# An encoder kernel on one core: pieces of turned heads issued by ScalarE, a query block moved ahead of the values, two more heads turned by DMA

## The chip, the cores and the metric

The kernel runs on one core of one Trainium2 chip. The metric is the device time of one execution in microseconds (us); lower is better. A core has TensorE (PE, with its weight loads PEld), VectorE (DVE), ScalarE (ACT), GpSimd (POOL) and SyncE (SP). Each takes its instructions in the order in which they were laid down, and waits on semaphores for the others. A DMA is issued by one of these instruction streams (here by SP, by POOL, and at the very end by ACT) and carried out by 16 DMA engines that all of them share. A row whose engine ends in "q" (SPq, ACTq) is the issuing itself, done by the engine's sequencer.

## The reference

Two encoder layers work on 256 tokens of width 2048. Both have four cross-attention heads into 256 memory tokens. The first layer has twelve heads of neighbourhood attention with a bias; the second has twelve query heads over four key and value heads, with queries and keys normalised per head and rotated by position. All of the changed parts lie in the attention of the two layers:

```
n = rms_norm(h, attn_norm[1])
z = n @ b_w_in[0]
q, k, v, qm = split(z)
q = axial_rope(rms_norm(split_heads(q, 12), b_q_norm[0]))
k = axial_rope(rms_norm(split_heads(k, 4), b_k_norm[0]))
mix = gqa_block_attention(q, k, v)            # softmax(q k^T / sqrt(128)) v per head
cross = memory_attention(qm, km, vm)          # four heads into the memory tokens
h = h + concat([mix, cross]) @ w_o[1]
h = h + square(relu(rms_norm(h, mlp_norm[1]) @ w_up[1])) @ w_down[1]
```

## The kernel before

**Products.** Every fp32 matrix is split into two parts, hi (ScalarE rounds it, line 330) and lo (VectorE subtracts, line 331), and each product is made of three TensorE matmuls: hi·hi, lo·hi, hi·lo (lines 238, 241, 242 for blocks of 512 columns; 250 to 252 and 823 to 825 for blocks of 256). Weights come in chunks of 1 MB, loaded by SP (line 186) into three buffers (`raw`) and split in two halves; four buffers hold the hi and lo halves.

**Order.** The work is a list of grains, one per half of a chunk. A counter ticks once per grain. `later(n, f)` runs `f` n ticks on, so that attention work is written between the grains of the projections. From this written order and its own estimates of durations a planner lays out the final order of the instructions on each engine; the instructions wrapped in `pin` keep their written order.

**Attention of one head** has three steps. `attend` makes the scores on TensorE (lines 393 to 395), the maximum on VectorE (404), the exponential on ScalarE (406) and the scaling on VectorE (411). The second step turns the probabilities. It has two forms: with `attend2`, TensorE transposes four 128x128 squares (436) and the result is split; with `turned`, VectorE transposes 32x32 squares (417) and `moved` writes four pieces to DRAM (line 382, one DMA for each group of 32 partitions) and reads them back in the wanted order with one DMA from POOL (383); `attend2_turned` splits what came back (330 and 331, tile `pT`). `attend3` multiplies by the values (444 to 446). A list such as `blocks=(0, 6, 8)` says how many ticks after its begin each step is written.

**Second layer.** The plan before is: the memory queries and the keys together, the values (block 4 of the weights), then three blocks of four query heads (0, 1, 2), then the output projection `add_o(1)`, then the MLP. `normed_heads` squares the sums on ScalarE with the row's factor (1199), gets the head's factor on VectorE and POOL (337, 339), multiplies it by the row's factor on POOL (1202), scales on ScalarE (1205) and rotates on VectorE (1207 to 1215). `heads_turned` turns queries or keys through `moved`; `heads_T` does it on TensorE (1169). `HEADS_AT` has the tick, counted from the end of a block, at which each of its four heads begins. Of block 0 all four heads are turned by DMA, of block 1 the first two, of block 2 none.

**Output projection.** `add_o` makes four blocks of 512 columns, two at a time, each a sum over four chunks of its input: chunk 3 has the memory heads, chunks 0, 1 and 2 have heads 0 to 3, 4 to 7 and 8 to 11.

`moved` has one more caller, `turned_rows`, which turns the rows of the activations ahead of and behind the MLP.

Of the kernel before, what the change touches and what calls it, by code (L numbers as in the profile page):

```python
# [17 lines left out]
P = 128  # L18
# [73 lines left out]
def encoder_kernel(ctx: ExitStack, tc: tile.TileContext, t: dict, out: bass.AP):  # L92
# [126 lines left out]
    def later(n, fn, *args):  # L219
        pending.append((state["tick"] + n, fn, args))  # L220
# [152 lines left out]
        return s  # L373


    def moved(dst, src):

        f = dst.shape[-1]
        x = dram.tile([P, 4, f], F32, tag=f"turn{f}", bufs=4, name="turn")
        to = x.rearrange("(b r) a f -> a r b f", r=32)  # L380
        for a in range(4):
            nc.sync.dma_start(to[a], src[32 * a : 32 * a + 32])
        nc.gpsimd.dma_start(dst, x)

    def scores(name):
# [28 lines left out]
    def turned(sc):  # L414

        x = scores("sc_t").rearrange("p a b -> p (a b)")
        nc.vector.transpose(x.rearrange("p (b k s j) -> p s k b j", b=4, k=2, s=2),
                            sc.rearrange("p s (k b r) -> p s k b r", k=2, b=4))
        back = sc.rearrange("p a b -> p (a b)").rearrange("p (a f) -> p a f", a=4)
        moved(back, x.rearrange("p (b f) -> p b f", b=4))  # L420
        return back

    def attend2_turned(back, o=0):
# [365 lines left out]
    def add_o(layer):  # L789
        first, second, third, late = 3, 0, 1, 2  # L790
        for n in (0, 2):
            if n:
                order = [(b, c) for b in range(2) for c in range(4)]
            elif layer:
                order = [(b, c) for c in (first, second, third, late) for b in range(2)]
            else:
                order = [(b, c) for b in range(2) for c in (first, second)]
                order += [(b, c) for c in (third, late) for b in range(2)]
            add_ms([([t[f"w_o{layer}"][nb * 4 + c] for c in range(4)], o_done(layer, nb)) for nb in (n, n + 1)],
                   parts_of("cat"), order)  # L800
            if n == 0 and layer == 1:
                last = [halves_of(w) for w in plan[-4:]]
                del plan[-4:]
                for two in (last[:2], last[2:]):
                    plan.extend(x[hf] for hf in range(2) for x in two)
# [280 lines left out]
    def down_done(layer, nb):  # L1086
        def f(w):
            for i in range(NT):
                add_scaled(h[:, i, nb * 512 : (nb + 1) * 512], w.ps[i], box["inv"][:, i : i + 1])
            for i in range(NT):  # L1090
                sum_squares(2 * layer + 1, i, nb)
            if layer == 1:
                later(1, times_gf, nb)
                return
            if nb == 0:
                box["nT"] = wide("nT1", 480)
            if nb == 3:
                closed("mlp")
                open_ring()
            later(1, turned_input, nb)  # L1100
            if nb == 3:

                def norm():
                    box["rstd"] = keep.tile([P, NT], F32, name="rstd1")
                    box["mean"] = mean_square(1, 4, "mean")
                    nc.gpsimd.tensor_tensor(box["rstd"], box["mean"], mhalf[:, :NT], op=ALU.pow)
                later(2, norm)
        return f

# [63 lines left out]
    def heads_turned(src, dst):  # L1173

        backs = []
        for i in range(NT):
            room = scores("h_t").rearrange("p a b -> p (a b)")
            nc.vector.transpose(room.rearrange("p (b k j) -> p k b j", b=4, k=4),
                                src[i].rearrange("p (k b r) -> p k b r", k=4, b=4))
            back = src[i].rearrange("p (a f) -> p a f", a=4)  # L1180
            moved(back, room.rearrange("p (b f) -> p b f", b=4))
            backs.append(back)

        def heads_landed():
            for i in range(NT):
                hi, lo = (dst[:, :, x * SEQ + i * P : x * SEQ + (i + 1) * P].rearrange("p k (a j) -> p k a j", a=4)
                          for x in range(2))
                split(hi, lo, backs[i].rearrange("p a (k j) -> p k a j", k=4))

        later(5, lambda: past(heads_landed, box["splits"][-1]))  # L1190

    def normed_heads(w):
        cg, sg = box["rope"]
        outs = []
        for i in range(NT):
            y2 = at.work.tile([P, 4, HD], F32, tag="b_y2", name="b_y2")
            ss = small.tile([P, 4], F32, tag="b_ss", name="b_ss")
            for j in range(4):
                nc.scalar.activation(y2[:, j, :], w.ps[i][:, j * HD : (j + 1) * HD], AF.Square,
                                     scale=box["rstd"][:, i : i + 1], accum_out=ss[:, j : j + 1])  # L1200
            r = rstd_of(ss, HD, "b_r")
            nc.gpsimd.tensor_scalar(r, r, box["rstd"][:, i : i + 1], None, op0=ALU.mult)
            y = at.work.tile([P, 4, HD], F32, tag="b_y", name="b_y")
            for j in range(4):
                nc.scalar.activation(y[:, j, :], w.ps[i][:, j * HD : (j + 1) * HD], AF.Copy, scale=r[:, j : j + 1])
            o = at.work.tile([P, 4, HD], F32, tag="b_o", bufs=3, name="b_o")
            nc.vector.tensor_tensor(o, y, cg[:, i, None, :].to_broadcast([P, 4, HD]), op=ALU.mult)
            yv = y.rearrange("p h (a b c) -> p h a b c", a=2, b=2)
            y2v = y2.rearrange("p h (a b c) -> p h a b c", a=2, b=2)
            sv = sg[:, i, :].rearrange("p (a b c) -> p a b c", a=2, b=2)  # L1210
            for a in range(2):
                for b in range(2):
                    nc.vector.tensor_tensor(y2v[:, :, a, b, :], yv[:, :, a, 1 - b, :],
                                            sv[:, None, a, b, :].to_broadcast([P, 4, 32]), op=ALU.mult)
            nc.vector.tensor_tensor(o, o, y2, op=ALU.add)
            outs.append(o.rearrange("p a b -> p (a b)"))
        return outs
# [8 lines left out]
        box["vb"] = values("values", "vb", 1)  # L1226
        put_values(box["vb"], w.ps, box["rstd"])

    HEADS_AT = (7, 9, 10, 12), (5, 6, 8, 9), (1, 3, 5, 6)

    def b_q_done(blk):
        def f(w):
# [4 lines left out]
            else:  # L1237
                later(1, heads_turned, outs, qT)
            kvs = [(blk * 4 + j) // (NH // NKV) for j in range(4)]
            jobs = [(qT[:, j, :], box["kT"][:, kv, :], None, head_of(box["vb"], kv), blk * 4 + j, box["cat"])  # L1240
                    for j, kv in enumerate(kvs)]
            n = (4, 2, 0)[blk]
            for j, job in enumerate(jobs):
                begin = HEADS_AT[blk][j]
                if j < n:
# [29 lines left out]
    for w in plan[-8:-5]:  # L1275
        w.early = True
    plan[-6].early = "last"
    add_m(blocks(4), parts_of("nT"), b_v_done)
    for blk in range(3):
        add_m(blocks(blk), parts_of("nT"), b_q_done(blk))  # L1280
    add_o(1)
    add_mlp(1)
# [131 lines left out]
```

## Time and profile before

| | |
|---|---|
| time, median of 3 runs | 2014.71 us (2011.62 to 2015.72) |
| time of the profiled execution | 2011.52 us |
| its span, first to last instruction | 2009.4 us |
| granted TensorE clock | 0.999 |
| busy: TensorE, VectorE, ScalarE, GpSimd | 1997.4, 1691.8, 1245.8, 142.7 us |

The shares of busy time are those of the whole span. The attention of the first layer lies between about 105 and 365 us, the projections and the attention of the second between about 1090 and 1290 us; the long stretches of MLP lie around them. The parts of the change touch only the two attention stretches.

### The profile page before, as it was taken

How to read it: one execution, taken by the hardware profiler on the slowest of the kernel's cores; microseconds unless marked ns; L12 is line 12 of the kernel's file. 1: busy time of each engine (PE TensorE's matmuls, PEld its weight loads, DVE VectorE, ACT ScalarE, POOL GpSimd, SP SyncE). 2: the span in 40 equal slices, each digit the busy share in tenths (PEclk: the TensorE clock that was granted, in tenths of full speed). 3: DMA queues.
4: the chain of work that ended last, by engine and by line, in shares of the span. 5: the costliest groups of instructions: out<-in, count | busy, mean ns of one | idle time of the engine just before them, and what ended most of it. 6: DMA issues, size and time to landing. Idle time of an engine off the chain costs nothing.

```text
span 2009.4 us, 32896 instructions
## 1 busy us (share of the span) xinstructions
PE 1997.4 (99%) x12945; PEld 1807.2 (90%) x12945; DVE 1691.8 (84%) x2080; ACT 1245.8 (62%) x1650; POOL 142.7 (7%) x185
## 2 busy tenths in 40 slices
PE   9999999999999999999999999999999999999998
PEld 8999999899999999999988888889999999999997
DVE  6767767669998999999998778768989999999896
ACT  6755555557666666666655567657666666666664
POOL 0000000000000000000000112000000000000000
PEclk9999999999999999999999999999999999999999
DMA  7766666847777787787767776557777777777763
GB/s 286 300 224 217 219 222 210 329 134 236 223 232 232 233 233 235 217 244 236 216 215 262 257 260 213 216 190 239 227 231 223 235 229 234 225 239 231 235 224 115
DMA packets 121626, 461.13 MB, mean 229 GB/s; under 512 B 13824, under 2 KB 36992, under 8 KB 88320
## 3 DMA queue, kind: packets, MB, share of 16 engines
q1 hardware_dynamic: 100080, 412.90, 61.3%
q0 software_dynamic: 20816, 45.10, 10.5%
q8 instruction: 101, 1.65, 0.3%
q10 hardware_dynamic: 576, 1.05, 0.1%
q14 instruction: 53, 0.43, 0.1%
HBM read 411.80 MB, written 17.83 MB: 214 GB/s over the span
## 4 chain that ended last, share of the span: by engine, by line
PE 94%; DMA 2%; DVE 2%; issue 1%; ACT 1%; SPq 0%; POOLq 0%; POOL 0%; DVEq 0%; ACTq 0%
PE ps_u L825 12%; PE ps_u L824 12%; PE ps_u L823 12%; PE p L942 9%; PE p L941 9%; PE p L940 9%; PE ps_m L242 7%; PE ps_m L238 7%; PE ps_m L241 7%; PE ps_s L250 3%; PE ps_s L252 3%; PE ps_s L251 3%; DMA sc<-turn 1%; DVE lo L331 1%; DMA raw<-in_w_o 1%
## 5 line engine op out<-in xcount | busy, mean ns | idle before, releaser
L825 PE MATMUL ps_u<-hT,ul 128*128 128x256 f32 x2048 | 566.4, 277 | 0.0
L824 PE MATMUL ps_u<-hT,uh 128*128 128x256 f32 x2048 | 565.1, 276 | 0.0
L823 PE MATMUL ps_u<-hT,uh 128*128 128x256 f32 x2048 | 564.5, 276 | 0.0
L330 ACT ACTIVATE uh<-raw_U 128x1024 fp32r<-128x1024 f32 x278 | 294.5, 1061 | 297.8 <-PE ps_u L824 280.3
L824 PEld LDWEIGHTS ps_u<-hT,uh 128*128 128x128 f32 x2048 | 384.3, 188 | 6.6
L823 PEld LDWEIGHTS ps_u<-hT,uh 128*128 128x128 f32 x2048 | 384.2, 188 | 5.6
L825 PEld LDWEIGHTS ps_u<-hT,ul 128*128 128x128 f32 x2048 | 384.3, 188 | 0.1
L331 DVE TENSOR_TENSOR ul<-raw_U,uh 128x1024 fp32r<-128x1024 f32 x278 | 337.6, 1219 | 25.5 <-ACT uh L330 25.5
L331 DVE TENSOR_TENSOR lo<-raw,hi 128x1024 fp32r<-128x1024 f32 (+1 forms) x224 | 265.1, 1191 | 102.5 <-ACT hi L330 99.9
L330 ACT ACTIVATE hi<-raw 128x1024 fp32r<-128x1024 f32 (+1 forms) x224 | 230.4, 1038 | 166.3 <-PE ps_m L242 65.7
L330 ACT ACTIVATE th<-t 128x2048 fp32r<-128x2048 f32 x112 | 215.1, 1921 | 115.4 <-PE p L942 108.8
L331 DVE TENSOR_TENSOR tl<-t,th 128x2048 fp32r<-128x2048 f32 x112 | 256.2, 2288 | 28.1 <-ACT th L330 27.4
L331 DVE TENSOR_TENSOR bl<-b,bh 128x1536 fp32r<-128x1536 f32 x112 | 196.3, 1753 | 5.3 <-ACT bh L330 5.3
L330 ACT ACTIVATE bh<-b 128x1536 fp32r<-128x1536 f32 x112 | 166.7, 1488 | 19.4 <-PE p L942 13.2
L920 POOL DMA_DIRECT2D t<-b x112 | 96.5, 861 | 1126.0 <-DVE t L919 419.7
L942 PE MATMUL p<-th,a_s 128*128 128x512 f32 x448 | 176.3, 393 | 0.0
L941 PE MATMUL p<-tl,a_s 128*128 128x512 f32 x448 | 176.0, 393 | 0.0
L940 PE MATMUL p<-th,a_s 128*128 128x512 f32 x448 | 159.1, 390 | 0.0
L942 PE MATMUL p<-bh,a_s 128*128 128x512 f32 x336 | 131.7, 392 | 0.0
L941 PE MATMUL p<-bl,a_s 128*128 128x512 f32 x336 | 131.1, 390 | 0.0
L251 PE MATMUL ps_s<-nT,hi 128*128 128x256 f32 x448 | 124.1, 277 | 0.0
L250 PE MATMUL ps_s<-nT,hi 128*128 128x256 f32 x448 | 123.9, 277 | 0.0
(288 smaller groups left out, 3790.0 us busy)
## 6 DMA issues: line engine op xcount, KB each, us to landing
raw_U<-in_w_up SPq DMA_DIRECT2D x128, 1024.0 KB, 7.5
b<-in_w_pair SPq DMA_DIRECT2D x112, 768.0 KB, 4.9
raw<-in_w_o SPq DMA_DIRECT2D x32, 1024.0 KB, 5.6
t<-in_w_pair SPq DMA_DIRECT2D x112, 256.0 KB, 3.3
t<-b POOLq DMA_DIRECT2D x112, 256.0 KB, 7.3
raw<-in_w_b SPq DMA_DIRECT2D x21, 1024.0 KB, 5.9
raw<-in_w_av SPq DMA_DIRECT2D x12, 1024.0 KB, 5.1
raw<-in_w_aq SPq DMA_DIRECT2D x12, 1024.0 KB, 5.1
```

Source lines behind the costliest of these rows:

```text
L238: first = nc.tensor.matmul(w.ps[i], ah, hi[:, s], start=st, stop=False)
L241: nc.tensor.matmul(w.ps[i], ah, lo[:, s], start=False, stop=False)
L250: nc.tensor.matmul(ps, hi[:, s], acts[:, k, :SEQ], start=k == 0, stop=False)
L251: nc.tensor.matmul(ps, hi[:, s], acts[:, k, SEQ:], start=False, stop=False)
L330: first = nc.scalar.activation(dst_hi, src, AF.Copy)
L331: return first, nc.vector.tensor_tensor(dst_lo, src, dst_hi.bitcast(F32), op=ALU.subtract)
L823: nc.tensor.matmul(ps, hi[:, s], acts[:, k, :SEQ], start=k == 0, stop=False)
L824: nc.tensor.matmul(ps, hi[:, s], acts[:, k, SEQ:], start=False, stop=False)
L825: nc.tensor.matmul(ps, lo[:, s], acts[:, k, :SEQ], start=False, stop=k == KT - 1)
L940: nc.tensor.matmul(ps, a[:, 0, ai, :], hi[:, s], start=begins, stop=False)
L941: nc.tensor.matmul(ps, a[:, 0, ai, :], lo[:, s], start=False, stop=False)
L942: nc.tensor.matmul(ps, a[:, 1, ai, :], hi[:, s], start=False, stop=ends)
```

## The change

Five things are changed together.

1. `moved` takes a queue. `turned` and `heads_turned` give it ScalarE's, so the four pieces of every turned head, query and key are issued by ScalarE; `turned_rows` keeps SP. The read back stays with POOL.
2. In the second layer query block 0 is projected ahead of the values (block 4). Since the values do not exist yet when its heads are written, they are looked up when the third step runs (`values_of`).
3. In block 1 all four heads are turned by DMA (before: two), and they begin at ticks 1, 3, 5, 7 instead of 5, 6, 8, 9.
4. `normed_heads` squares without the row's factor. The small constant of the norm is multiplied by the row's mean square once (`least`), so that the head's factor comes out whole and the multiplication on POOL (1202) is gone.
5. The first two blocks of the second layer's output projection take their first two chunks as in the first layer: both chunks of one block, then both of the other, instead of alternating.

```diff
-    def moved(dst, src):
+    def moved(dst, src, queue=nc.sync):
...
-            nc.sync.dma_start(to[a], src[32 * a : 32 * a + 32])
+            queue.dma_start(to[a], src[32 * a : 32 * a + 32])
         nc.gpsimd.dma_start(dst, x)
...
-        moved(back, x.rearrange("p (b f) -> p b f", b=4))
+        moved(back, x.rearrange("p (b f) -> p b f", b=4), nc.scalar)
...
-            elif layer:
-                order = [(b, c) for c in (first, second, third, late) for b in range(2)]
             else:
                 order = [(b, c) for b in range(2) for c in (first, second)]
                 order += [(b, c) for c in (third, late) for b in range(2)]
...
+                    box["least"] = keep.tile([P, NT], F32, name="least")
+                    nc.vector.tensor_scalar(box["least"], box["mean"], EPS, None, op0=ALU.mult)
...
-            moved(back, room.rearrange("p (b f) -> p b f", b=4))
+            moved(back, room.rearrange("p (b f) -> p b f", b=4), nc.scalar)
...
-                                     scale=box["rstd"][:, i : i + 1], accum_out=ss[:, j : j + 1])
-            r = rstd_of(ss, HD, "b_r")
-            nc.gpsimd.tensor_scalar(r, r, box["rstd"][:, i : i + 1], None, op0=ALU.mult)
+                                     accum_out=ss[:, j : j + 1])
+            v = small.tile([P, 4], F32, tag="rs_v", name="b_r_v")
+            nc.vector.tensor_scalar(v, ss, 1.0 / HD, box["least"][:, i : i + 1], op0=ALU.mult, op1=ALU.add)
+            r = small.tile([P, 4], F32, tag="rs_r", name="b_r_r")
+            nc.gpsimd.tensor_tensor(r, v, mhalf[:, :4], op=ALU.pow)
...
-    HEADS_AT = (7, 9, 10, 12), (5, 6, 8, 9), (1, 3, 5, 6)
+    HEADS_AT = (7, 9, 10, 12), (1, 3, 5, 7), (1, 3, 5, 6)
+
+    def values_of(kv):
+        return lambda part, kt: head_of(box["vb"], kv)(part, kt)
...
-            jobs = [(qT[:, j, :], box["kT"][:, kv, :], None, head_of(box["vb"], kv), blk * 4 + j, box["cat"])
+            jobs = [(qT[:, j, :], box["kT"][:, kv, :], None, values_of(kv), blk * 4 + j, box["cat"])
...
-            n = (4, 2, 0)[blk]
+            n = (4, 4, 0)[blk]
...
+    add_m(blocks(0), parts_of("nT"), b_q_done(0))
     add_m(blocks(4), parts_of("nT"), b_v_done)
-    for blk in range(3):
+    for blk in range(1, 3):
         add_m(blocks(blk), parts_of("nT"), b_q_done(blk))
```

## The prediction

> **What bounds the kernel now.** I read the page first: which engine is full, and who carries the chain that ended last.
>
> ```profile
> PE 1997.4 (99%) x12945; PEld 1807.2 (90%) x12945; DVE 1691.8 (84%) x2080; ACT 1245.8 (62%) x1650; POOL 142.7 (7%) x185
> PE 94%; DMA 2%; DVE 2%; issue 1%; ACT 1%; SPq 0%; POOLq 0%; POOL 0%; DVEq 0%; ACTq 0%
> ```
>
> TensorE is busy for 1997.4 us of a span of 2009.4 us, and 94% of the chain is TensorE. So 12 us are the most that could be saved without taking work from it. Next come its waits in the whole span, to see where these 12 us lie.
>
> ```profile
> PE unread L136 <- POOL idle L133: 1.3, 1, 1.3
> ...
> PE pt_h L1169 <- DVE b_o L1215: 0.3, 1, 0.3
> PE ps_m L241 <- DVE lo L331: 0.2, 1, 0.2
> ```
>
> Only the last two lie in the attention of the second layer; the rest is the start, and the tail behind the last matmul, which the change leaves alone. Then the windows of the stages: length, PE, PEld, DVE, ACT and POOL busy, clock, DMA share.
>
> ```profile
> 120.00:400.00 280.00, 279.94 (x1902) 257.31 (x1902) 198.17 (x294) 148.37 (x249) 9.33 (x17) 1.00 0.70 238
> 1152.00:1232.00 80.00, 80.00 (x393) 67.61 (x392) 62.81 (x112) 51.32 (x126) 12.75 (x18) 1.00 0.73 239
> 1208.00:1256.00 48.00, 47.45 (x253) 39.86 (x251) 44.97 (x93) 34.74 (x93) 9.16 (x12) 1.00 0.69 220
> ```
>
> In the first layer's attention TensorE is full. In the second it is full too, but for 0.55 us near 1248, where VectorE is at 94% (44.97 of 48). That crowd is the only place where the kernel waits for what the change moves.
>
> A busy TensorE can hide small gaps, since a matmul counts beyond the start of the next. So I read the starts there.
>
> ```profile
> 1247.59 0.62 PE L238 MATMUL ps_m<-hi,cat 128*128 128x512 f32 x2
> 1248.50 0.87 PE L1169 MATMUL pt_h<-ident,b_o 128*128 128x128 f32 x6 [0.29 <-DVE b_o L1215]
> 1249.13 0.48 PE L242 MATMUL ps_m<-hi,cat 128*128 128x512 f32 x1
> 1249.83 0.50 PE L241 MATMUL ps_m<-lo,cat 128*128 128x512 f32 x1 [0.22 <-DVE lo L331]
> 1250.17 0.40 PE L242 MATMUL ps_m<-hi,cat 128*128 128x512 f32 x1
> 1250.40 0.40 PE L238 MATMUL ps_m<-hi,cat 128*128 128x512 f32 x1
> ...
> 1253.68 0.60 PE L436 MATMUL pt_a<-ident,sc 128*128 128x128 f32 x4
> 1254.04 0.36 PE L393 MATMUL sc_ps<-kT,qT 128*128 128x256 f32 x1
> 1254.24 0.28 PE L394 MATMUL sc_ps<-kT,qT 128*128 128x256 f32 x1
> ...
> 1255.58 0.39 PE L241 MATMUL ps_m<-lo,cat 128*128 128x512 f32 x1
> 1256.07 0.73 PE L242 MATMUL ps_m<-hi,cat 128*128 128x512 f32 x2
> ...
> 1257.34 0.39 PE L241 MATMUL ps_m<-lo,cat 128*128 128x512 f32 x1
> 1257.72 0.39 PE L444 MATMUL av<-pT,vb 128*128 128x256 f32 x1
> ```
>
> From 1250.17 to 1250.40 one matmul of 512 columns takes 0.23 us. Beyond that, 1247.59 to 1248.50 holds 0.45 us of nothing (two matmuls, 0.46, in 0.91), 1249.13 to 1249.83 0.47, 1255.58 to 1256.07 0.26, 1257.34 to 1257.72 0.15: together **1.3 us**.
>
> **The change, part by part.**
>
> *Two more heads turned by DMA.* Eight transposes leave TensorE. Four start in 0.36 us (1253.68 to 1254.04), and the matmul behind them is followed after 0.20 instead of 0.12 us: 0.44 for four, so two heads give **-0.9 us**. VectorE gets two transposes more, priced below, in exchange for no other work; TensorE never waits for them if they have the six ticks that the plan leaves. If they are late, the third step stands in TensorE's queue and everything behind it waits; that price is inside the cases below.
>
> *Block 0 ahead of the values, block 1 earlier.* The head factors show when a block is through:
>
> ```profile
> 1133.94 2.02 POOL L339 TENSOR_TENSOR b_r_r<-b_r_v,mhalf 128x4 f32<-128x4 f32 x2
> 1180.57 1.04 POOL L339 TENSOR_TENSOR b_r_r<-b_r_v,mhalf 128x4 f32<-128x4 f32 x1 [2.45 <-DVE b_r_v L337]
> 1206.36 1.04 POOL L339 TENSOR_TENSOR b_r_r<-b_r_v,mhalf 128x4 f32<-128x4 f32 x1 [6.20 <-DVE b_r_v L337]
> ```
>
> Keys at 1134, block 0 at 1181, block 1 at 1206: a block is some 25 us. Block 0 then ends near 1156 and its four heads work from about 1170 to 1212 instead of from 1207 to 1245, out of the crowd. The last of block 1 is as late as before, but two ticks thinner. The 1.3 us of gaps are bounded by 0 (the crowd stays) and -1.3; I take all, **-1.3 us**, because the four heads that leave are a third of the second layer's query heads, and VectorE missed by only half a microsecond.
>
> *The weight loads.* SP now waits with the weights behind pieces:
>
> ```profile
> 1238.57 9.50 SPq L382 DMA_DIRECT2D turn<-sc_t  x8
> 1248.16 0.44 SPq L186 DMA_DIRECT2D raw<-in_w_o  x1
> 1253.50 1.06 ACT L330 ACTIVATE hi<-raw 128x1024 fp32r<-128x1024 f32 x1 [2.38 <-DMA raw<-in_w_o]
> ```
>
> A weight left at 1248.16, after eight pieces had held the queue for 9.5 us, and ScalarE had to wait for it until 1253.50. This goes. It is one of the causes of the 1.3 us and is not counted again. What is next in the load's way is the freeing of a `raw` buffer by VectorE.
>
> *Norms.* The POOL multiplication, the wider scalar operand on VectorE and `least` shift fractions of a microsecond on engines with room, outside the one gap at 1248.50, already counted: 0. Without that cover the whole of it is below 1 us.
>
> *Order of the projection.* The same matmuls; the second pair of sums starts two grains later, so the last block's sums have longer to be read. 0, since no wait names it; the weights wanted first are in the same queue order.
>
> *The issuing, on ScalarE.* This is the part that can cost. What one issue takes, on SP and on ScalarE:
>
> ```profile
> L382 SPq DMA_DIRECT2D turn<-sc_t x104: 302/432/1397, 113.9 to 1247.6; - x104
> 1997.50 1.34 ACT L1132 ACTIVATE h<-h,fin_r 128x512 f32<-128x512 f32 x2 [1.15 <-POOL fin_r L339]
> 1998.26 0.95 ACTq L1135 DMA_DIRECT2D out<-h  x2
> ```
>
> 0.43 us on SP, 0.48 on ScalarE (0.95 for two). ScalarE's first issue began at 1998.26, while its activation ran to 1998.84: the end of a running activation hides part of it. Moved are 28 turned heads (16, 12) and six halves of queries and keys, 34 x 4 = 136 issues, 65 us of ScalarE's stream. Ahead of each group it may also have to sit out VectorE's transpose, and then its splits queue up behind, for which TensorE waits in the end.
>
> First layer: 16 heads, 64 issues, 31 us, on top of 148.37 in 280: 64% busy, no bound. But the pieces may leave later, and some heads have little room between the turned tile and its first product:
>
> ```profile
> 140.79 0.69 DVE L331 TENSOR_TENSOR pT<-sc,pT 128x512 fp32r<-128x512 f32 x1 [2.41 <-ACT pT L330]
> 140.81 0.39 PE L444 MATMUL av<-pT,vm 128*128 128x256 f32 x1
> ...
> 289.14 0.69 DVE L331 TENSOR_TENSOR pT<-sc,pT 128x512 fp32r<-128x512 f32 x1 [2.94 <-ACT pT L330]
> 290.12 0.28 PE L444 MATMUL av<-pT,vl 128*128 128x256 f32 x1
> ```
>
> These are the first and the last of four heads with under 1 us. Below, the bound is 0: earlier pieces give nothing to a full TensorE. Above, each of the four is late by one whole split of 1.06 us: 4.2. I take the mean: ScalarE is busy 53% of the time, half a split is 0.53 us, so 0.28 for each of four, **+1.1 us**.
>
> Second layer, 1152 to 1232: ScalarE has 51.3 us. Four heads' `pT` and output splits come in, some 4.7 us (0.63 and about 0.55 each). Issues: 8 for the queries of block 0, 16 for the memory heads, 16 for block 0, 8 to 16 for block 1, so 48 to 56, by 0.43 to 0.48: 21 to 27 us. The sum is 77 to 83 of 80 us if nothing overlaps; with half an activation (0.3 us) hidden in each of 12 to 14 groups, 73 to 79. That is close. What protects TensorE is that the splits run ahead:
>
> ```profile
> ACT hi L330 <- PE ps_m L242: 65.7, 48, 3.0
> L330 ACT ACTIVATE hi<-raw 128x1024 fp32r<-128x1024 f32 (+1 forms) x224 | 230.4, 1038 | 166.3 <-PE ps_m L242 65.7
> ```
>
> ScalarE waits 48 times for TensorE to free a half: it has four halves, three of them ahead, each 12 matmuls of 0.23, so 8.3 us, less about 2.3 for the split itself. A lead of 6 us absorbs short holds. I take **0** here; the upper end is the rival's.
>
> *The sum.* -0.9 - 1.3 + 1.1 = -1.1 us, for the profiled execution 2011.5 - 1.1 = 2010.4. The median of the runs, 2014.71, stands 3.2 us above that execution, so the forecast for the median is **2013.6 us**.
>
> **Rivals.** *ScalarE becomes the bound (slower).* In 1152 to 1232, 83 us of work and issues, and waits in front of VectorE's transposes:
>
> ```profile
> L417 DVE STREAM_TRANSPOSE sc_t<-sc x26: 702/710/714, 113.1 to 1244.8; 128x512 f32<-128x512 f32 x26
> ```
>
> 14 groups of 0.71 are 9.9, so 93 of 80 us: 13 too many, less the lead of 6: +7, or +13 where the lead is used up already. It decides from the point where ScalarE's share of that window exceeds one. For it: the sum is within 10% of the window. Against it: ScalarE idles 36% there now, the planner sees the issues, and holds shorter than the lead cost nothing. Time 2013.6 + 7 = 2020.6, up to 2026.6.
>
> [...]
>
> *The change doesn't do what it says.* The planner lays the issues behind ScalarE's splits, the pieces leave a microsecond later, the heads are only shifted, and the crowd near 1248 stays: the transposes' -0.9 remain against +1.1 to +4.2. That is 2014.9 to 2018.0.
>
> *Clearly faster.* It would take 4 us. TensorE has only 2.2 to give here; a larger gain needs gaps that the starts don't show. Time 2010 or less.
>
> **Chances.** A measurement of this kernel can tell about 0.2%, 4 us, from no change: faster is below 2010.7, slower above 2018.7. Forecast 0.48, shift without gain 0.20, ScalarE as the bound 0.22 (the lock's extra in 0.04 of it), clearly faster 0.10. Nearly the whole of the bound's share is slower, and 0.01 of the shifted case. So faster 0.10, same 0.67, slower 0.23. The forecast's own range is 2010.5 (nothing lost in the first layer, and the spread of the runs shown, which begin at 2011.62) to 2017. To leave out no more than 2 in 10 I reach to 2009.3 and, into the bound's case, to 2021.
>
> **What would show it.** Right: eight fewer TensorE transposes at line 436, no wait of TensorE near 1248, SP without pieces of heads, ScalarE below 95% in any 40 us of the second attention, TensorE's waits under 2 us in both. Wrong: waits of TensorE for `hi` or `lo` between 1150 and 1235 with ScalarE full; waits of the value products for `pT` in the first layer of over 2 us; issues on ScalarE well above 0.48 us.

## The result, and the profile after

| | before | after |
|---|---|---|
| time, median | 2014.62 us | 2087.48 us |
| lowest to highest | 2011.62 to 2015.72 | 2085.34 to 2098.29 |
| span of the profiled execution | 2009.4 us | 2086.5 us |
| granted TensorE clock | 0.999 | 0.994 |

The ratio is 1.0377, with an interval of 1.0345 to 1.0409: **slower by some 73 us** where 1 us less was forecast. The page of after, engines and chain:

```profile
PE 2044.2 (98%) x12937; PEld 1847.1 (89%) x12937; DVE 1697.0 (81%) x2085; ACT 1241.0 (59%) x1652; POOL 135.8 (7%) x179
PE 85%; DMA 7%; DVE 3%; ACT 2%; issue 1%; ACTq 1%; POOLq 0%; SPq 0%; DVEq 0%
```

Two things stand out. DMA, 2% of the chain before, has 7%: TensorE waits for transfers. And TensorE itself is busy for 47 us *more* with eight instructions fewer: its matmuls have become longer. ScalarE's busy time is that of before (1241.0 against 1245.8), but the 136 issues that it got are not counted in it. The waits of TensorE in after:

```profile
PE av L444 <- ACT pT L330: 23.5, 12, 4.3
PE ps_m L238 <- ACT hi L330: 2.2, 2, 1.3
PE ps_m L241 <- DVE lo L331: 1.6, 2, 1.0
```

The first line did not exist before. 22.1 of its 23.5 us lie before 380 us, in the first layer. To place the rest I cut the span into stages at the starts of TensorE's matmuls. The first layer's projections, with the attention written between them, are the matmuls of `ps_s` on `nT`. Columns: count, duration min/median/max in ns, first and last start. Before:

```profile
L250 PE MATMUL ps_s<-nT,hi x448: 276/276/287, 97.3 to 335.8; 128*128 128x256 f32 x150
```

and after:

```profile
L250 PE MATMUL ps_s<-nT,hi x448: 277/281/420, 98.3 to 377.8; 128*128 128x256 f32 x150
```

The stage takes 41 us longer (279.5 against 238.5), and the median matmul in it takes 281 ns instead of 276. Cut in the same way, the stages of all kernels are, in us (output 1 ends with the first up product, `ps_u`; MLP 1 with the first projection of the second layer; attention 2 is the second layer's projections, attention and output projection, up to the last matmul of `ps_m` in it; the rest is everything behind):

| kernel | attention 1 | output 1 | MLP 1 | attention 2 | rest | median time |
|---|---|---|---|---|---|---|
| before | 238.5 | 79.9 | 673.5 | 248.1 | 672.1 | 2014.62 |
| after | 279.5 | 80.8 | 684.2 | 260.4 | 683.3 | 2087.48 |
| e1 queue only | 274.4 | 79.2 | 673.5 | 257.2 | 673.3 | 2059.26 |
| e2 all but queue | 246.7 | 79.8 | 684.2 | 248.3 | 685.8 | 2044.96 |
| e3 tile only | 246.7 | 79.8 | 684.2 | 250.6 | 684.0 | 2047.19 |
| e4 no new tile | 277.1 | 81.2 | 673.6 | 264.1 | 672.9 | 2064.44 |
| e5 no queue, no tile | 238.3 | 79.8 | 673.6 | 245.6 | 675.3 | 2012.59 |
| e6 tile, MLP moved back | 246.7 | 79.8 | 673.7 | 250.4 | 674.0 | 2024.86 |
| e7 third step later | 263.1 | 84.4 | 673.6 | 257.2 | 672.9 | 2054.00 |
| e8 first layer by SP | 238.3 | 79.8 | 673.5 | 260.8 | 672.9 | 2024.09 |
| e9 issued twice | 240.0 | 80.0 | 673.8 | 274.6 | 672.0 | 2041.57 |
| e10 both steps later | 252.7 | 79.4 | 676.2 | 257.7 | 672.9 | 2037.93 |
| e11 memory heads too | 246.0 | 78.9 | 676.2 | 264.2 | 672.9 | 2033.68 |
| e12 old projection order | 238.3 | 79.8 | 673.5 | 248.9 | 673.4 | 2013.47 |
| e13 tile of 64 bytes | 245.3 | 79.9 | 677.4 | 248.7 | 676.4 | 2025.88 |
| e14 tile of 96 bytes | 248.4 | 79.9 | 684.1 | 250.4 | 682.4 | 2046.99 |

The median times come from several measurements, in which before had medians of 2011.57 to 2014.62 us; ratios are always to the before measured beside a kernel. The stages are those of one profiled execution each. Attention 2 varies most: the six kernels that share it (after, e4, e7, e8, e10, e11) have 257.2 to 264.2 us there. The loss has three places: attention 1 (+41.0), attention 2 (+12.3), and both MLPs (+10.7 and +11.2), where the change edits nothing at all. That its parts touch only the two attention stretches, as was said ahead of the prediction, holds for the edits and not for what they move.

### The profile page after: what moved, and what is told of

Same layout as the page of the kernel before. It is cut to its first block, busy times and chain, and to the rows that moved or that the text cites. A ratio compares the mean times of both kernels' runs of the same rounds, so it can differ in the third digit from the quotient of the medians.

```text
span 2086.5 us, 32865 instructions
## 1 busy us (share of the span) xinstructions
PE 2044.2 (98%) x12937; PEld 1847.1 (89%) x12937; DVE 1697.0 (81%) x2085; ACT 1241.0 (59%) x1652; POOL 135.8 (7%) x179
## 4 chain that ended last, share of the span: by engine, by line
PE 85%; DMA 7%; DVE 3%; ACT 2%; issue 1%; ACTq 1%; POOLq 0%; SPq 0%; DVEq 0%
PE ps_u L822 12%; PE ps_u L821 11%; PE ps_u L823 11%; PE p L940 9%; PE p L938 9%; PE p L939 9%; PE ps_m L241 5%; PE ps_m L238 5%; PE ps_m L242 5%; DMA sc<-turn 4%; PE ps_s L250 2%; PE ps_s L251 2%; PE ps_s L252 2%; DMA turn<-sc_t 1%; DVE lo L331 1%
## 5 line engine op out<-in xcount | busy, mean ns | idle before, releaser
L821 PE MATMUL ps_u<-hT,uh 128*128 128x256 f32 x2048 | 574.1, 281 | 1.1 <-ACT c L878 1.1
L822 PE MATMUL ps_u<-hT,uh 128*128 128x256 f32 x2048 | 574.2, 281 | 0.7 <-DVE hT L357 0.7
L823 PE MATMUL ps_u<-hT,ul 128*128 128x256 f32 x2048 | 574.6, 281 | 0.0
L821 PEld LDWEIGHTS ps_u<-hT,uh 128*128 128x128 f32 x2048 | 391.2, 191 | 6.7 <-ACT c L878 1.3
L822 PEld LDWEIGHTS ps_u<-hT,uh 128*128 128x128 f32 x2048 | 385.1, 188 | 7.1 <-DVE hT L357 0.9
L251 PE MATMUL ps_s<-nT,hi 128*128 128x256 f32 x448 | 128.2, 286 | 0.0
L250 PE MATMUL ps_s<-nT,hi 128*128 128x256 f32 x448 | 128.2, 286 | 0.0
```

Of the source, the lines that this page charges most:

```text
L250: nc.tensor.matmul(ps, hi[:, s], acts[:, k, :SEQ], start=k == 0, stop=False)
L251: nc.tensor.matmul(ps, hi[:, s], acts[:, k, SEQ:], start=False, stop=False)
L821: nc.tensor.matmul(ps, hi[:, s], acts[:, k, :SEQ], start=k == 0, stop=False)
L822: nc.tensor.matmul(ps, hi[:, s], acts[:, k, SEQ:], start=False, stop=False)
L823: nc.tensor.matmul(ps, lo[:, s], acts[:, k, :SEQ], start=False, stop=k == KT - 1)
```

## The experiments

### Which part costs: e1, e2, e3, e4, e5

e1 is before with ScalarE's queue alone; e2 is after without it:

```diff
+        moved(back, x.rearrange("p (b f) -> p b f", b=4), nc.scalar)          # e1, with the queue argument, both callers
-        moved(back, x.rearrange("p (b f) -> p b f", b=4), nc.scalar)          # e2, both callers
+        moved(back, x.rearrange("p (b f) -> p b f", b=4))
```

> The kernel before, with the pieces of turned heads, queries and keys issued by ScalarE and nothing else changed. Theory: the loss has two sources, the issuing by ScalarE (in the two attention stretches, +42 and +12 us after the change) and the 32 bytes of the new tile, which shift all tiles of the left side and slow the matmuls everywhere (+22 us in the two MLPs, some 5 more in the attention). Then this gives 2014.7 + 37 to 49, so 2052 to 2064 us, with the MLPs as long as before (673 us each). Rival, the issuing alone is behind everything, the MLPs too: 2080 to 2090 us.

> The changed kernel with the pieces issued by SP as before. Theory: the wait of TensorE for turned heads in the first layer goes, the shift by 32 bytes stays: 2014.7 + 27, so 2037 to 2045 us, with MLPs of 684 us. Rival, the issuing alone: 2011 to 2016 us.

Measured: e1 1.0233 of before (1.0211 to 1.0256), e2 1.0165 (1.0148 to 1.0182). Neither part is harmless. In the table e1 loses in the attentions and nothing in the MLPs; e2 loses where the matmuls are longer. e3 adds to before only the 32 bytes a partition and the one VectorE operation; e4 is after without the tile, its values kept in the tile `x_mean`, which is dead by then; e5 is e4 with the pieces issued by SP:

```diff
+                    box["least"] = keep.tile([P, NT], F32, name="least")      # e3, on before
+                    nc.vector.tensor_scalar(box["least"], box["mean"], EPS, None, op0=ALU.mult)
...
-                    box["least"] = keep.tile([P, NT], F32, name="least")      # e4 and e5, on after
+                    box["least"] = box["x_mean"]
```

> The kernel before with the new 32-byte tile and the one VectorE operation that fills it, which nothing reads: the order of TensorE's instructions in the attention is that of before, the tiles of the left side lie 32 bytes further on. Theory (addresses): 2036 to 2045 us, the 256-column matmuls at 281 ns instead of 276. Rival (the planner's order or the issuing slows the MLP): 2014 to 2016 us.

> The changed kernel, but the small constant of the norm is put into a tile that is no longer read, so no tile moves. Theory: the MLPs are back at 673 us each and the attention stretches keep most of their loss: 2087.5 - 27, so 2055 to 2066 us. Rival (the issuing alone): 2085 to 2090 us.

> The changed kernel without its two suspects: the pieces are issued by SP, and the small constant lies in a tile that is no longer read, so no tile moves. Theory: the rest of the change (block 0 first, four heads of block 1 turned by DMA, norms, order of the projection) is worth what the first prediction worked out for it, -0.9 - 1.3 us: 2008 to 2011 us where the kernel before has 2011.7. Rival: these parts cost something in the second layer as well, 2014 to 2020 us.

Measured: e3 1.0171 (1.0156 to 1.0186), e4 1.0253 (1.0227 to 1.0279), e5 1.0001 (0.9991 to 1.0011). So the tile alone costs as much as all of e2, the queue as much as all of e4, and **everything else in the change is worth nothing** within 0.1%, 2 us. (e5 lies 1.6 us above the range that its parts were given.) The two costs add up to somewhat more than the change's. In attention 1 they are 8.2 and 38.6 us apart and 41.0 together; that slower matmuls fill some of the waits is the likely reason, not shown.

### The tile: e6, e13, e14

`least` is allocated ahead of most working tiles, so all behind it lie 32 bytes further on. Counted in the laid-out programs, the weights' halves `hi` and `lo` and the tile `cat` go from 128 to 160 bytes past a multiple of 256, the MLP's tiles (`a_s`, `th`, `tl`, `bh`, `bl`, `z`, `c`) from 64 to 96; `nT` and `hT` (160) and `uh`, `ul` (224) stay. The kernel has constants for such places (`MLP_AT`, `PLAIN_AT`, `STILL_AT`, `MOVING_AT`), which say that they had been chosen. What the matmuls do with that, in e3's groups by shape (count, busy us and mean ns), is seen in three windows of the first MLP: from 424 to 480 us (the first row), from 480 to 500, where the first down products come in (two rows), and from 500 to 560:

```profile
L823 PE MATMUL ps_u<-hT,uh 128*128 128x256 f32 x130 | 35.7, 276 | 0.0
...
L823 PE MATMUL ps_u<-hT,uh 128*128 128x256 f32 x31 | 8.7, 280 | 0.0
L940 PE MATMUL p<-th,a_s 128*128 128x512 f32 x8 | 3.1, 390 | 0.0
...
L823 PE MATMUL ps_u<-hT,uh 128*128 128x256 f32 x96 | 27.0, 281 | 0.0
```

The up products read `hT` and `uh`, which have not moved. They run at 276 ns until the first products on *moved* tiles have run between them, and at 281 from there on. They then start 0.118 us apart instead of 0.113 (medians); 6144 of them (3 x 2048) by 4 to 5 ns would be 25 to 31 us, and the two MLP columns of e3 show 22.6. The first of MLP 1 still run at the old pace; those of the second MLP are slow from its start (281 ns in e3 from 1350 to 1400 us). e6 takes the MLP's tiles back, by making the gap ahead of them smaller; the attention's stay moved:

```diff
-MLP_AT = 192
+MLP_AT = 160
```

> The kernel of the pad alone (the new 32-byte tile in the kernel before), with the gap ahead of the MLP's tiles made 32 bytes smaller, so that the tiles of the MLP lie where they lay before and those of the attention stay shifted. In the pad's trace the up products go from 276 to 281 ns right behind the first down products, though their own operands lie where they lay. Theory (the address of the down products' operands sets the pace of what follows): MLPs of 673 us again, 2047 - 22, so 2022 to 2028 us. Rival (something else that the tile changes slows the up products): 2044 to 2049 us.

Measured 1.0056 (1.0041 to 1.0072). MLP 1 and the rest are back at 673.7 and 674.0 us (673.5 and 672.1 before), while attention 1 keeps its 246.7. The up products of e6:

```profile
L823 PE MATMUL ps_u<-hT,uh x2048: 275/276/386, 424.6 to 1966.4; 128*128 128x256 f32 x187
```

So it is the place of the tiles, not the tile or its operation. e13 and e14 make the tile 64 and 96 bytes long, to find which property of the place counts:

```diff
-                    box["least"] = keep.tile([P, NT], F32, name="least")
+                    box["least"] = keep.tile([P, 16], F32, name="least")[:, :NT]   # e13; 24 in e14
```

> As e3_pad (before, with the new tile and its one VectorE operation), but the tile is 64 bytes a partition instead of 32, so everything behind it moves by 64 bytes. If matmuls slow down when their weights and their moving tile start at the same place modulo 64 bytes, this keeps the places apart, and the matmuls go at 276 ns again: 2010-2015 us, ratio 0.998 to 1.002. If any move away from the tuned place modulo 256 costs, it stays at 2030-2048 us. If the tile or its operation itself cost, 2047 us.

> As e13_pad_64 with a tile of 96 bytes: a move that shares the place modulo 64 again, as 32 bytes do, at other places modulo 256. If the place modulo 64 decides, it is as slow as e3_pad: 2040-2050 us, ratio 1.014 to 1.019, matmuls of 256 columns at 281 ns. If the place modulo 256 decides (the splits at 160 as nT is, in e3_pad), it lies elsewhere: 2012-2030 us.

Measured: e13 1.006 (1.0043 to 1.0077), e14 1.0168 (1.0152 to 1.0184). The MLPs bear out the place modulo 64 for the most part (677.4 and 676.4, with a median of 276 ns, against 684.1 and 682.4 at 281). Attention 1 doesn't: with 64 bytes it is as slow as with 32 and 96 (245.3, 246.7, 248.4). Neither rule fits both stages, and e13's time lies between the ranges that the two rules gave. That the places of these tiles cost 1.7% here is shown (e3 and e6, and e2 against e5). Which of the tiles counts (`z` and `c` are no operands of a matmul) and by what rule is left open. The place isn't all of it either: in e5, where no tile moved, the up products of the second MLP run at 281 ns too, until its first down products (see e12).

### The queue in the first layer: e8, e9, e7, e10, e11

e8 is e4 with SP's queue in the first layer alone, ScalarE's in the second:

```diff
-                    res = turned(res)
+                    res = turned(res, nc.scalar if "rope" in box else nc.sync)
```

> No new tile; the pieces of the first layer are issued by SP, those of the second by ScalarE. Theory: the first layer is as long as before, the second keeps its loss of 10 to 12 us: 2020 to 2025 us. Rival (nothing in the second layer comes from the issuing): 2009 to 2013 us.

Measured 1.0055 (1.0037 to 1.0073); attention 1 is back at 238.3 us. Of e4's loss 38.8 us are the first layer's queue. Is it the time that issuing takes from ScalarE? In after one issue takes 452 ns (the middle of min/median/max), as predicted:

```profile
L382 ACTq DMA_DIRECT2D turn<-sc_t x112: 309/452/1987, 115.0 to 1321.7; - x112
```

e9 pays that time without relying on it: e5, in which ScalarE issues each piece once more, into a scratch tile nobody reads, while SP's pieces stay the ones in use.

```diff
+        if twice:
+            y = dram.tile([P, 4, f], F32, tag=f"copy{f}", bufs=4, name="copy")
+            to = y.rearrange("(b r) a f -> a r b f", r=32)
+            for a in range(4):
+                nc.scalar.dma_start(to[a], src[32 * a : 32 * a + 32])
```

> The kernel of run e5 (pieces by SP, no new tile), and ScalarE issues every piece a second time, into memory that nothing reads: the 136 issues and their waits for VectorE's transposes are on ScalarE, but the path of a turned head stays on SP. Theory one (ScalarE's time for the issues and the waits ahead of them cost the 40 us of the first layer): 2045 to 2065 us. Theory two (the laid-down order is at fault, which lets ScalarE and TensorE reach the turned tile before it is back): 2012 to 2025 us.

Measured 1.0139 (1.0124 to 1.0155), but attention 1 takes 240.0 us: +1.7, with all of ScalarE's issues in it, though ScalarE's own stream was held for those copies often there (waits of ScalarE, 98 to 360 us; us in total, times, longest):

```profile
ACT cat L330 <- DMA copy<-sc_t: 39.6, 7, 7.2
...
ACT kT L330 <- DMA copy<-sc_t: 20.3, 6, 4.1
```

(The planner laid e9's order anew as well, with 15.3 to 21.6 us of matmuls between a window head's scores and its value products.) The issuing time by itself isn't the first layer's loss.

e9 also shows issues of two engines at the same time. There SP and ScalarE issue side by side, and one issue takes hardly longer for it (1.82 and 1.94 us for four pieces, against 1.82 on SP alone in before and 1.81 on ScalarE alone in e4):

```profile
120.66 1.82 SPq L382 DMA_DIRECT2D turn<-sc_t  x4
120.66 1.94 ACTq L387 DMA_DIRECT2D copy<-sc_t  x4
```

Of ScalarE's 136 issues in e9, 111 overlap one of SP in time, with a median of 0.444 us (0.452 in after). In many groups ScalarE's last piece starts later, so four take up to 7 us; that is a wait ahead of an issue, and what it waits for was not followed up.

What the first layer's loss is, one window head shows. Before, from VectorE's transposition to the value product:

```profile
168.41 0.71 DVE L417 STREAM_TRANSPOSE sc_t<-sc 128x512 f32<-128x512 f32 x1
169.16 1.82 SPq L382 DMA_DIRECT2D turn<-sc_t  x4
173.78 0.55 POOL L383 DMA_DIRECT2D sc<-turn  x1 [32.09 <-DMA turn<-sc_t]
...
178.23 0.19 ACT L406 ACTIVATION_READ_ACCUMULATOR sc<-sc,nm 128x1 f32 x1
178.50 0.63 ACT L330 ACTIVATE pT<-sc 128x512 fp32r<-128x512 f32 x1
...
181.06 0.28 PE L444 MATMUL av<-pT,va 128*128 128x256 f32 x1
```

and the same head in e4:

```profile
176.87 0.71 DVE L417 STREAM_TRANSPOSE sc_t<-sc 128x512 f32<-128x512 f32 x1
177.62 1.81 ACTq L382 DMA_DIRECT2D turn<-sc_t  x4
182.09 0.55 POOL L383 DMA_DIRECT2D sc<-turn  x1 [31.52 <-DMA turn<-sc_t]
...
187.79 0.63 ACT L330 ACTIVATE pT<-sc 128x512 fp32r<-128x512 f32 x1 [5.12 <-DMA sc<-turn]
...
188.47 0.38 PE L444 MATMUL av<-pT,va 128*128 128x256 f32 x1 [1.96 <-ACT pT L330]
```

The pieces leave no later behind the transposition (0.04 us after its end in both) and take as long to issue (1.82, 1.81); the read back starts 4.66 and 4.51 us after the transposition. But ScalarE now *sits at* `pT` for 5.12 us, with nothing to do until the read back lands, where before it was busy until 178.42 and waited less than 0.1 us. Its stream has fewer weight splits ahead of `pT`, and TensorE's fewer matmuls ahead of the value product. Counted in the laid-out programs (the planner makes the order anew when an issue changes engine): in before and e8, the window heads' value products stand 16.4 to 19.7 us of matmuls behind their scores, in e1, e4 and after 13.6 to 17.7. Three of every four heads have some 3 us less room. The transfers are longer as well: from the end of the transposition to `pT`, which starts within 0.1 us of the landing in every head, the median of the heads is 8.7 us in before and e5, 8.8 in e8, and 10.1 to 10.3 in e1, e4 and after (9.38 and 10.21 in the head shown). Why they are longer is not shown.

In the four memory heads the room isn't less (17.4 to 19.7 us before, 18.4 to 20.2 in e4), and yet one of them has the longest wait, 4.3 us. There the pieces do leave late. The second of them in e4:

```profile
119.05 0.71 DVE L417 STREAM_TRANSPOSE sc_t<-sc 128x512 f32<-128x512 f32 x1
123.73 0.63 ACT L330 ACTIVATE pT<-sc 128x512 fp32r<-128x512 f32 x1 [4.19 <-DMA sc<-turn]
123.73 1.81 ACTq L382 DMA_DIRECT2D turn<-sc_t  x4
```

The transposition ends at 119.76, but ScalarE stands at the `pT` of the head before until that has landed, and issues only then: 3.97 us late. Before, SP issued these pieces 0.03 us behind the transposition.

e7, e10 and e11 widen the room by hand, on e4. e7 and e10 change the twelve window heads, e11 the four memory heads as well; `held` puts the second step behind the newest weight split:

```diff
-                      blocks=(0, 4, 5))
+                      blocks=(0, 4, 9))                  # e7: only the third step later
+                      blocks=(0, 8, 10), held=True)      # e10: second and third
...
-                      blocks=(0, 6, 8), held=True)       # e11: the memory heads, on e10
+                      blocks=(0, 8, 10), held=True)
```

> ScalarE issues as in the changed kernel, no new tile, but the third step of a head of the first layer is written at tick 9 instead of 5. In TensorE's order the value products then stand 20 to 25 us of matmuls behind the scores (13.6 to 17.7 before this edit, 16.4 to 19.7 in the kernel before the change). Theory (the planner puts the products too early, since it thinks that pieces from ScalarE are back sooner): the waits for the turned tile in the twelve window heads go, and most of the 41 us of the first layer: 2064 - 30, so 2025 to 2040 us. Rival (ScalarE is held by the issuing, and its splits are late): 2060 to 2068 us.

> Pieces by ScalarE as in the changed kernel, no new tile, and in the first layer's twelve window heads both later steps are put back: the split of the turned tile stands 4 or 5 weight splits behind the exponential in ScalarE's order (3 in the changed kernel, 3 or 4 in the kernel before), the value products 21 to 26 us of matmuls behind the scores. Theory one (time for the issues): 2045 to 2060 us, hardly below the 2054 of run e7. Theory two (order): ScalarE no longer sits in front of tiles on their way, and of the first layer's loss only that of the four memory heads stays: 2024 + 4 to 10, so 2026 to 2036 us.

> As e10_both_steps_later, but the four memory heads of the first layer, too, ask for their second and third steps two and two later (8 and 10 instead of 6 and 8), so that their value products stand 21.5 to 24.5 us of matmuls behind the scores instead of 18.4 to 20.2 and the split of the turned tile four weight splits behind the exponential instead of three. If the first layer's loss is the laid-down order, most of the 9 us that e10 still loses at 138 to 164 us goes: the first projection stage from 252.7 to 241-246 us, the time from 2037.9 to 2026-2032 us. If those heads are late for another reason (the transfers, or ScalarE's issuing), it stays at 2036-2039 us.

Measured: e7 1.02 (1.0175 to 1.0225), e10 1.0123 (1.0106 to 1.014), e11 1.009 (1.0071 to 1.0108); attention 1 goes from 277.1 to 263.1, 252.7 and 246.0 us. (The times of all three lie above the ranges that were expected of the order alone, e7's by 14 us, the others' by 2.) TensorE's waits in that stage, in e4 and behind it in e7:

```profile
PE av L444 <- ACT pT L330: 23.3, 10, 4.3
```

```profile
PE av L444 <- ACT pT L330: 5.5, 2, 4.2
PE sc_ps L393 <- ACT kT L330: 5.5, 6, 1.4
PE ps_m L241 <- DVE lo L331: 4.7, 8, 1.2
```

e7 loosens TensorE's order alone: TensorE waits far less for `pT`, but ScalarE still does, and what queues up behind it is late next (`kT`, and `lo`, which VectorE makes from ScalarE's `hi`). With ScalarE's order loosened too, 24.4 us come back in all, and 6.7 more with the memory heads: **31 of 38.8**, with ScalarE's queue still in use. 7.7 us stay, not taken apart further. ScalarE's own waits at `pT` hardly shrink, which e10 had expected. From 98 to 380 us they are, in before, e4 and e10:

```profile
ACT pT L330 <- DMA sc<-turn: 25.0, 11, 4.9
ACT pT L330 <- DMA sc<-turn: 63.4, 14, 6.9
ACT pT L330 <- DMA sc<-turn: 57.1, 15, 8.2
```

So standing at a landing isn't the loss by itself: e10 has 57.1 us of it, with attention 1 24.4 us shorter than in e4. It cost where TensorE had too little ahead of what stood behind it. The profiled execution of e11 is its slowest (2037.03 us, of 2028.25 to 2037.03); it has 264.2 us in attention 2 against e10's 257.7, with nothing changed there, and this hides most of the 6.7 us.

Why 23.3 us of waits cost 38.8 is seen in after, behind the longest of them (windows: busy us of PE, PEld, DVE, ACT, POOL, clock, DMA share, GB/s):

```profile
154.00:156.00 2.00, 0.00 (x0) 0.00 (x0) 0.00 (x0) 0.15 (x1) 0.00 (x0) 0.98 0.48 197
156.00:158.00 2.00, 1.47 (x7) 1.48 (x8) 1.49 (x3) 2.00 (x4) 0.00 (x0) 0.50 0.00 0
158.00:160.00 2.00, 2.00 (x11) 2.00 (x11) 1.86 (x4) 1.98 (x5) 0.00 (x0) 0.50 0.00 0
160.00:162.00 2.00, 2.00 (x11) 2.00 (x11) 1.61 (x4) 0.47 (x2) 0.00 (x0) 0.50 0.56 143
162.00:164.00 2.00, 2.00 (x16) 2.00 (x15) 0.25 (x1) 0.00 (x0) 0.00 (x0) 0.82 0.92 385
```

TensorE has waited 4.26 us; the granted clock is then 0.50 from 156 to 162 us, where TensorE does 11 matmuls in 2 us, and 16 in the window where the clock comes back (19 in the next). In e4's attention 1, windows of 4 us show a mean clock below 1.00 at six places; taken as time at 0.50, that is one stretch of 6.9 us and five of 3.4 us. By estimate these 24 us cost at most 12 at half speed, and with 23.3 us of waits that is up to 35 of the 38.8. What decides when the clock falls, and for how long, is not shown: from 186 to 190 us TensorE stands still for 1.96 us in e4, and the clock is 1.00 there and in the window behind.

### The queue in the second layer: e8 and e9 again

e8 has the fast first layer and still 260.8 us in attention 2, 15.2 more than e5. Some 2.4 of these come from where the stage ends, at the last matmul of the projection: e8's planner puts 21 up products of 0.113 us ahead of it, e5's none. In time e8 is 11.5 us above e5 (2024.09 against 2012.59). The granted clock and the engines from 1110 to 1290 us, e5 first, then e8:

```profile
1110.00:1290.00 180.00, 179.93 (x898) 151.80 (x897) 143.32 (x270) 113.20 (x278) 18.22 (x26) 1.00 0.69 226
```

```profile
1110.00:1290.00 180.00, 172.47 (x834) 143.35 (x833) 137.08 (x263) 106.27 (x271) 19.08 (x26) 0.98 0.64 211
```

ScalarE isn't full: its 106 us, and even with some 0.45 for each of 72 issues, stay well below 180. In the window of the prediction, 1152 to 1232, e8 has:

```profile
1152.00:1232.00 80.00, 75.49 (x353) 61.75 (x352) 62.42 (x119) 49.01 (x129) 11.13 (x15) 0.98 0.70 224
```

That is 49.01 us of ScalarE and 44 issues, some 20 us: 69 of 80 even if nothing overlaps. What delays TensorE is the order in its stream. e8's timeline:

```profile
1171.17 1.07 ACT L330 ACTIVATE hi<-raw 128x1024 fp32r<-128x1024 f32 x1 [1.66 <-PE ps_m L242]
1175.21 0.63 ACT L330 ACTIVATE pT<-sc 128x512 fp32r<-128x512 f32 x1 [2.97 <-DMA sc<-turn]
...
1176.62 4.21 ACTq L382 DMA_DIRECT2D turn<-h_t  x5
1180.88 0.48 ACT L406 ACTIVATE sc<-sc_ps,nm 128x256 f32<-128x256 f32 x1 [4.12 <-DMA turn<-h_t]
...
1181.79 1.05 ACT L330 ACTIVATE hi<-raw 128x1024 fp32r<-128x1024 f32 x1
...
1182.89 0.73 PE L238 MATMUL ps_m<-hi,nT 128*128 128x512 f32 x2 [0.88 <-ACT hi L330]
1184.66 0.79 PE L241 MATMUL ps_m<-lo,nT 128*128 128x512 f32 x1 [1.04 <-DVE lo L331]
1185.25 0.63 PE L242 MATMUL ps_m<-hi,nT 128*128 128x512 f32 x1
```

Between the split of 1171.17 and the next, of 1181.79, lie 2.97 us at `pT` and 4.12 behind five pieces of queries. The 6 us of lead are gone, TensorE runs dry, and its next matmuls of 512 columns take 0.63 us and more instead of 0.39: the granted clock is down here too (0.79 from 1182 to 1190 us). e9 points the same way from the other side: with each piece issued once more by ScalarE, and SP's in use, attention 2 takes 274.6 us, and the time is 29 us above e5's, between the ranges of both its theories. In the dense second layer ScalarE's holds cost; in the first the like ones cost 1.7. How much of it is e9's new order isn't separated.

### The projection order: e12

e5 gains 2.5 us in attention 2 and loses 3.2 behind it. (Before has 7 up products, 0.8 us, ahead of the last matmul of the projection, e5 none: counted alike, it gains 1.7 and loses 2.4.) There its up products run at 281 ns from 1335 to 1390 us, until the first down products come:

```profile
L823 PE MATMUL ps_u<-hT,ul 128*128 128x256 f32 x144 | 40.1, 281 | 0.0
```

e12 is e5 with the old order of the output projection:

```diff
+            elif layer:
+                order = [(b, c) for c in (first, second, third, late) for b in range(2)]
```

> As e5_no_queue_no_tile (all of the change but the queue and the new tile), with the second layer's output projection in the order of before again. In e5 the second layer's attention was 2.5 us shorter and the stretch behind it 3.2 us longer than before, its up products at 281 ns a matmul from 1335 to some 1390 us instead of 276. If the projection's order set that pace, the stretch behind the attention goes back from 675.3 to about 672 us and the time is 2009-2010 us, about 0.997 to 0.999 of before, faster than both kernels. If something else sets it, the stretch stays at 675 us and the time at 2012-2013 us.

Measured 0.9999 (0.999 to 1.0008). The 0.997 to 0.999 that was hoped for isn't there. The rest falls to 673.4 and attention 2 grows to 248.9, but 2.4 us of this come from the stage's end again: e12 has 21 up products ahead of the projection's last matmul. The old order gains nothing. No kernel of this study beats before.

## Why the prediction was wrong

Step by step, as the prediction put it.

- **What bounds the kernel** was read rightly: TensorE is full, and nothing but TensorE's own work could be saved. It was not seen that a kernel so full has its whole loss ahead of it: any wait, and any nanosecond a matmul, counts in full.
- **Two more heads turned by DMA, and block 0 ahead** (-0.9 and -1.3): right in attention 2, where e5 gains some 1.7 us (2.5 in the table), no wait of TensorE is left between 1100 and 1300, and eight transposes at line 436 are gone (x24 before, x16 after). The gain is given back behind it (2.4 us), by the pace of the next matmuls, which the prediction had no term for.
- **Norms, "0", and below 1 us without cover: this step failed**, by some 34 us (e3), and not through its operations. `least` was priced by its work and not by its 32 bytes, which move the tiles of the projections and of the down products (e6). The constants for such places stood in the kernel.
- **Order of the projection, 0**: right in sum (e5 against e12).
- **The issuing, first layer, +1.1 with bounds of 0 and 4.2: this step failed**, by 38 us. It let pieces leave late, by at most one split, within the order of before. In the window heads the pieces left on time; what changed was the order, which the planner lays anew when an instruction changes engine, with some 3 us less room, and the transfer, which took some 1.4 us longer. In the memory heads pieces did leave late, by 3.97 us and not by a split of 1.06, since what held them was ScalarE's wait for a landing. The bound of "one whole split for each of four heads" thus bounded nothing: ten waits, up to 4.3 us each, and the clock at 0.50 behind some of them (six stretches in e4). The price of one issue (0.43 to 0.48) was right (0.452), and ScalarE's time was no limit, as said.
- **The issuing, second layer, 0: failed**; the rival "ScalarE becomes the bound" (+7 to +13) has the size, +11.5 in e8 against e5. But its mechanism is wrong: ScalarE never fills that window (at most 69 of the 80 us in e8). Single holds of 3 to 4 us in its order use up the lead of 6 us. That this rival's number fits is luck. The lock to which the chances give 0.04 is shown by no run: in e9 the issues of SP and ScalarE run side by side, at 0.444 us in the median.
- **What would show it**: the listed signs of "wrong" were the right ones. Waits of the value products for `pT` in the first layer are 22.1 us where 2 were the limit. Waits for `hi` and `lo` came without a full ScalarE.

## What to carry over

When a DMA changes its issuing engine under a planner, count the order of every engine again before pricing anything: the distance from a transfer's issue to its first use mattered more here (some 3 us less room, 1.4 us more to the landing) than the half microsecond of the issue, and an engine that executes in order shouldn't stand at a transfer's landing with work queued behind it that another engine needs soon. When TensorE is full, a new tile belongs in a dead one (e5), or, untested here, behind all others, since 32 bytes cost 34 us here. Look for constants that place tiles before adding one. Test each part of a bundle alone: here one part was worth nothing, and the two harmless-looking ones cost 34 and some 50 us.

## What was unexpected of the hardware

- **A matmul's pace changed here with what ran before it, and with where tiles lie.** In e3's first MLP, products on unmoved operands went from 276 to 281 ns after products on moved ones had begun, and stayed there; with the MLP's tiles back in place they ran at 276 ns (e6); in e5 they ran at 281 ns with nothing moved, until the first down products. The granted clock was 0.999 in the profiled executions of e3, e13 and e14 as in before's. The rule behind it is open (e13 and e14).
- **A wait of 4.26 us was followed by over 6 us at half the clock** (0.50 from 156 to 162 us in after), and e4's attention 1, with 23.3 us of waits and six stretches of lower clock, is 38.8 us longer than e5's.
- **Issues of SP and ScalarE side by side hardly lengthened each other here**: four pieces took 1.82 us on SP and 1.94 on ScalarE at the same time (e9), and the median of the overlapping issues was 0.444 us.
- **Moving an issue cost far more than the issue takes**: one takes 0.452 us on ScalarE in after, against 0.432 on SP in before; moving 136 of them costs some 50 us in total (e4 against e5), by order and holds.
